# Two feed-forward up projections written as 2x2 block products with seven multiplications

## The chip, the cores and the metric

The kernel runs on one core of one Trainium2 chip. The metric is the device time of one execution in microseconds, the median of several runs; one further execution was profiled, and all rows below come from that one. The core has five engines with a queue each: TensorE (PE, matmuls; its weight loads are listed apart as PEld), VectorE (DVE), ScalarE (ACT), GpSimd (POOL) and SyncE (SP, which here issues the transfers).

## The reference

The model is two layers of a first kind (attention, convolution and retention side by side, then a feed-forward part) followed by one layer of a second kind (differential attention, a state-space branch, then a gated feed-forward part), on one sequence of 512 tokens with width 1024, in float32. The change concerns the feed-forward parts of the second and of the last layer:

```python
# first kind, second layer (D_FF = 4096)
h = rms_norm(x, g_mlp_pre)
f = jnp.square(jax.nn.relu(h @ w_up)) @ w_down
return x + rms_norm(f, g_mlp_post)

# second kind, the last layer (D_FF_2 = 2816)
hn = rmsnorm(h, norm2_gain[i])
up = causal_dwconv(hn @ w_up[i], conv_w[i], conv_b[i])   # 3 taps along the tokens
gate, val = jnp.split(up, 2, axis=-1)
h = h + (jax.nn.silu(gate) * val) @ w_down[i]
```

## The kernel before

All matmuls work on numbers of 128x128 weights by up to 512 columns in the type fp32r. Each float32 operand is split in two such numbers, `hi` (a rounded copy, made by ACT or DVE) and `lo` (the rest, a subtraction, made by DVE or POOL), and a product is the sum of three matmuls: hi by hi, hi by lo, lo by hi (`mm3`).

Weights come as one stream in a fixed order, in chunks of 128 x 1024 numbers (512 KB). A chunk is loaded by SP into a raw buffer (`wraw`, pool `wr`, four buffers), and split into `whi` and `wlo` (pools `wh` and `wl`, four pairs). Other tiles of 128 x 512 come from the pool `sp`. A chunk of an up projection holds 128 output columns for all eight blocks of 128 inputs; its unit (`f_unit`) is 8 x 3 = 24 matmuls of 512 columns (all tokens) into one PSUM bank, and the result has the features on the partitions. The first four units of a feed-forward part are cut in two halves of 256 tokens (`f_split`), so that the first half can run while the last tokens are still being normalised and transposed into `hhi` and `hlo` (`to_hT`). A down projection (`down`) takes four blocks of 128 hidden features at a time and adds 8 outputs (4 token blocks by 2 halves of the width), 12 matmuls of 512 columns each, to an accumulator in SBUF (`acc`, in the last layer the residual `X` itself). So a group of four hidden blocks in the second layer is 4 x 24 + 96 = 192 matmuls, and in the last layer, where every hidden block has a gate and a value unit, 8 x 24 + 96 = 288.

No order is written out by hand beyond that. The program records every operation with a due time (`prio`; evacuations get an earlier one), and `Trace.order` then replays the recording with a table of costs: it picks for each engine the available operation that is due first, chooses among engines where there is a choice (`copy`: ACT or DVE; `sub`: DVE or POOL, with a bias in ns that the stage sets through `wbias`; a bias of 100000 ns keeps POOL out), and takes buffers from the pools. What comes out is a fixed order for each engine. All instructions are issued from one helper line, so every row of the profile has the line L642 (L674 in the changed kernel), and rows are told apart by their tiles.

In the rows, `ps` is a PSUM bank, `t`, `cu` and `cv` are results of up units, `fhi` and `flo` the split hidden features, `st` a column of statistics.

Of the kernel before, what the change touches and what calls it, by code (L numbers as in the profile page):

```python
# [17 lines left out]
P = 128  # L18
S = 512
# [26 lines left out]

def mlp_groups():
    return [(4 * g, 4) for g in range(NG1)]


def ffn2_groups():
    n = DFF2 // 128
    return [(k, min(4, n - k)) for k in range(0, n, 4)]
# [6 lines left out]
def stream_spec():  # L60
    out = []
    for l in range(LAYERS):
# [12 lines left out]
        gs = mlp_groups()  # L75
        for g, (k0, n) in enumerate(gs):
            out += [f_chunk("w_up", l, 128 * (k0 + i)) for i in range(n)]
            if g:
                out += down_chunks("w_down", l, *gs[g - 1])
        out += down_chunks("w_down", l, *gs[-1])  # L80
# [19 lines left out]
    gs = ffn2_groups()  # L100
    for g, (k0, n) in enumerate(gs):
        for i in range(n):
            out.append(f_chunk("w_up_2", 0, 128 * (k0 + i)))
            out.append(f_chunk("w_up_2", 0, DFF2 + 128 * (k0 + i)))
        if g:
            out += down_chunks("w_down_2", 0, *gs[g - 1])
    out += down_chunks("w_down_2", 0, *gs[-1])
# [292 lines left out]
class Trace:  # L400
# [247 lines left out]
    def sub(self, out, a, b, bias=1):  # L648
# [3 lines left out]
        return self.add(alts, (out, a, b), {"op": ALU.subtract})  # L652
# [119 lines left out]

class Side:
# [35 lines left out]
class Builder:  # L809
# [3 lines left out]
    NR, NW = 4, 4  # L813
# [6 lines left out]
    def __init__(self, tc, ctx, A, out):  # L820
# [8 lines left out]
        self.sp = pool("sp", 79 - 2 * self.NR - 4 * self.NW, [P, 512])  # L829
# [8 lines left out]
        self.wbias = 2  # L838

# [23 lines left out]
    def mm3(self, ps, w, a, start, stop):  # L863
        nc = self.nc
        (whi, wlo), (ahi, alo) = w, a
        nc.tensor.matmul(ps, whi, ahi, start=start, stop=False)
        nc.tensor.matmul(ps, whi, alo, start=False, stop=False)
        nc.tensor.matmul(ps, wlo, ahi, start=False, stop=stop)
# [116 lines left out]
    def to_hT(self, t, hs):  # L985
        nc = self.nc
        for h in range(2):
# [4 lines left out]
            self.split(ps.rearrange("p (k n) -> p k n", k=4), self.hhi[sl], self.hlo[sl])  # L992
# [349 lines left out]
    def hybrid(self, l):  # L1342
# [86 lines left out]
        self.side.drain()  # L1429
        self.finish(lambda t: (p0[t],), 4, W_OUT_KS, mix, X, gpost, gpre)  # L1430
        self.mix = {}
        self.mlp(l, X)
# [17 lines left out]
    def mlp(self, l, X):  # L1450
# [35 lines left out]
        self.finish_mlp(groups[-1], lhs, acc, X, gpost, gpre, store)  # L1486
        self.xd = xd

    def down(self, grp, lhs, acc, f, first):
        nc = self.nc  # L1490
        k0, n = grp
        nch = n // 2
        ks = list(range(k0, k0 + n))
        for h in range(2):
            ws = [self.ws.take() for _ in range(nch)]
            for t in range(NT):
                ps = self.ps()
                for c in range(nch):
                    self.t_part(ps, ws[c], ks[2 * c:2 * c + 2], t, 512, lhs, c == 0, c == nch - 1)
                if first:  # L1500
                    if h == 0:
                        acc[t] = [None, None]
                    acc[t][h] = self.s2(name="acc")
                    nc.scalar.copy(acc[t][h], ps)
                else:
                    nc.vector.tensor_tensor(acc[t][h], ps, acc[t][h], op=ALU.add)
        for k in ks:
            f.pop(k)

    def finish_mlp(self, grp, lhs, acc, X, gpost, gpre, store):  # L1510
# [6 lines left out]
        for t in range(NT):  # L1517
# [9 lines left out]
            store(t)  # L1527
        self.pending = hs
# [330 lines left out]
    def second(self):  # L1859
# [139 lines left out]
        hs = {}  # L1999
        for t in range(NT):  # L2000
# [11 lines left out]
    def ffn2(self, X):  # L2012
        nc = self.nc
        f, tg = {}, {}
        self.wbias = 3
        cw, cb = PV["convw2"][0], PV["convb2"][0]

        def unit(i, val):
            c = i + (22 if val else 0)

# [18 lines left out]
        for g, (k0, n) in enumerate(groups):  # L2039
# [4 lines left out]
            for u in us:  # L2044
                self.f_unit(u)
# [42 lines left out]
```

## Time and profile before

| | |
|---|---|
| median of 3 runs | 2135.91 us (2134.16 to 2139.28) |
| the profiled execution | 2135.72 us, of which the span from the first to the last instruction is 2134.0 us |
| TensorE matmuls busy | 2036.2 us (95%) |
| VectorE, ScalarE, GpSimd busy | 1362.7, 931.8 and 727.8 us |
| second layer's feed-forward part | from 907.9 to about 1267.8 us |
| last layer's feed-forward part | from 1767.4 us to the end |

The table is read from the top: the span is the time from the first instruction to the last, a busy time is the union of the recorded instructions of an engine, and the two lower lines say where in the span the stages lie that the change touches. The recorded length of a matmul is longer than its distance to the next one, since matmuls overlap in the array; what a matmul costs is the distance between two starts.

### The profile page before, as it was taken

To read this page: it belongs to the slowest core of one execution; us is meant where nothing else is said; L and a number is where in the kernel's file an instruction comes from. 1 tells how busy PE (TensorE), PEld (TensorE's weight loads), DVE (VectorE), ACT (ScalarE), POOL (GpSimd) and SP (SyncE) were. 2 spreads that over 40 slices of the span, in tenths; PEclk is the share of its full clock that TensorE was granted. 3 is DMA by queue.
4 is the path that set the end of the run, shared out by engine and by line. 5 is a ranking of instruction groups with operands and counts; after the bars stand their busy time and mean duration, and the time that the engine had idled before them with its cause. 6 is when DMAs were issued, how large, how long until landed. Compare 5 with 4: busy or idle time off the path is not lost. (4 is left out here: it accounts for less than half of the span.)

```text
span 2134.0 us, 27037 instructions
## 1 busy us (share of the span) xinstructions
PE 2036.2 (95%) x9964; PEld 1709.2 (80%) x9964; DVE 1362.7 (64%) x2127; ACT 931.8 (44%) x1527; POOL 727.8 (34%) x858
## 2 busy tenths in 40 slices
PE   7999889999999998899999998999999999999999
PEld 7987788778888977688888887677777788888887
DVE  5998795444457998563445473379888546655545
ACT  3377544222234376543233244457568224333322
POOL 3662367970004662300000035854553431000000
PEclk9999999999999999999999999999999999999999
DMA  5423333333242423222333354322324423333322
GB/s 181 129 60 119 109 103 130 111 117 99 79 126 90 129 72 116 79 90 89 98 90 108 99 186 139 91 85 65 98 82 146 164 88 100 99 99 99 97 81 79
DMA packets 85556, 225.16 MB, mean 106 GB/s; under 512 B 10416, under 2 KB 20400, under 8 KB 85424
## 3 DMA queue, kind: packets, MB, share of 16 engines
q1 hardware_dynamic: 85424, 223.43, 32.9%
q8 instruction: 79, 1.29, 0.3%
q14 instruction: 53, 0.43, 0.1%
HBM read 204.25 MB, written 19.14 MB: 105 GB/s over the span
## 5 line engine op out<-in xcount | busy, mean ns | idle before, releaser
L642 POOL TENSOR_TENSOR wlo<-wraw,whi 128x1024 fp32r<-128x1024 f32 (+1 forms) x156 | 367.1, 2361 | 1066.9 <-ACT whi L642 865.7
L642 ACT CAST whi<-wraw 128x1024 fp32r<-128x1024 f32 (+1 forms) x323 | 330.8, 1031 | 702.7 <-PE ps L642 617.8
L642 PE MATMUL ps<-hhi,whi 128*128 128x512 f32 (+1 forms) x1488 | 502.7, 367 | 8.7 <-DVE acc L642 2.8
L642 PE MATMUL ps<-hlo,whi 128*128 128x512 f32 (+1 forms) x1488 | 501.7, 367 | 6.8 <-DVE hlo L642 6.8
L642 PE MATMUL ps<-hhi,wlo 128*128 128x512 f32 (+1 forms) x1488 | 501.4, 366 | 0.4 <-DVE wlo L642 0.3
L642 PEld LDWEIGHTS ps<-hhi,whi 128*128 128x128 f32 x1488 | 273.5, 191 | 52.7 <-issue 5.1
L642 PEld LDWEIGHTS ps<-hlo,whi 128*128 128x128 f32 x1488 | 273.8, 192 | 49.3 <-DVE hlo L642 7.9
L642 PEld LDWEIGHTS ps<-hhi,wlo 128*128 128x128 f32 x1488 | 273.4, 191 | 43.4 <-DVE wlo L642 1.4
L642 DVE TENSOR_TENSOR wlo<-wraw,whi 128x1024 fp32r<-128x1024 f32 x178 | 224.6, 1263 | 109.2 <-ACT whi L642 109.1
L642 PE MATMUL ps<-whi,fhi 128*128 128x512 f32 x688 | 249.0, 391 | 5.1 <-DVE acc L642 2.8
L642 PE MATMUL ps<-whi,flo 128*128 128x512 f32 x688 | 249.3, 390 | 0.0
L642 PE MATMUL ps<-wlo,fhi 128*128 128x512 f32 x688 | 249.2, 391 | 0.0
L642 DVE TENSOR_TENSOR acc<-ps,acc 128x512 f32<-128x512 f32 x112 | 76.5, 687 | 153.0 <-PE ps L642 153.0
L642 PE MATMUL ps<-wlo,hhi 128*128 128x384 f32 (+1 forms) x448 | 157.6, 371 | 3.8 <-POOL wlo L642 3.8
L642 PE MATMUL ps<-whi,hhi 128*128 128x384 f32 (+1 forms) x448 | 155.7, 371 | 0.9 <-ACT whi L642 0.7
L642 PEld LDWEIGHTS ps<-whi,fhi 128*128 128x128 f32 x688 | 129.5, 188 | 32.6 <-DVE acc L642 3.2
L642 PE MATMUL ps<-whi,hlo 128*128 128x384 f32 (+1 forms) x448 | 155.3, 370 | 0.0
L642 PEld LDWEIGHTS ps<-whi,flo 128*128 128x128 f32 x688 | 129.7, 189 | 27.1
L642 PEld LDWEIGHTS ps<-wlo,fhi 128*128 128x128 f32 x688 | 129.8, 189 | 26.9
L642 POOL TENSOR_TENSOR st<-st,mhalf 128x1 f32<-128x1 f32 (+1 forms) x56 | 54.8, 980 | 194.0 <-DVE st L642 192.0
L642 DVE TENSOR_SCALAR t<-ps 128x512 f32<-128x512 f32 x64 | 44.1, 690 | 87.9 <-PE ps L642 87.9
L642 DVE TENSOR_TENSOR X<-ps,X 128x512 f32<-128x512 f32 x56 | 38.6, 689 | 91.7 <-PE ps L642 91.7
(249 smaller groups left out, 3247.5 us busy)
## 6 DMA issues: line engine op xcount, KB each, us to landing
wraw<-in_wst SPq DMA_DIRECT2D x302, 512.0 KB, 3.5
wraw<-in_wst SPq DMA_DIRECT2D x32, 384.0 KB, 3.1
gain<-in_gains SPq DMA_DIRECT2D x20, 256.0 KB, 4.3
X<-in_x SPq DMA_DIRECT2D x16, 256.0 KB, 5.4
xd<-X SPq DMA_DIRECT2D x16, 256.0 KB, 2.0
X<-xd SPq DMA_DIRECT2D x16, 256.0 KB, 5.5
gated<-t SPq DMA_DIRECT2D x16, 256.0 KB, 2.1
gate<-gated SPq DMA_DIRECT2D x16, 256.0 KB, 3.6
```

What stands on the lines that cost most here:

```text
L642: getattr(getattr(self.nc, e), m)(*[r(x) for x in op.args], **{k: r(v) for k, v in op.kw.items()})
```

## The change

In both feed-forward parts, after the first four units, two neighbouring units become one `FastUp`: the second layer takes chunks 2i and 2i+1, the last layer the gate and the value chunk of block i. Weights are cut into 2x2 blocks (inputs 0 to 511 and 512 to 1023, by the two chunks), the activations too (the same two halves of the inputs, by tokens 0 to 255 and 256 to 511). Instead of eight block products there are seven (Winograd's form of Strassen's scheme), each 4 x 3 = 12 matmuls of 256 columns. What is then new:

* four sums of weights per pair of units (`wsum`, and `wraw` in place), each 128 x 512, and splits of 3 1/2 instead of 2 chunks (`take_fast`);
* once per stage, copies of the untransposed numbers (`rawT`), eight sums of activations (`sraw`) and their splits (`fast_in`), one of them written over the second token half of `hhi` and `hlo`;
* two PSUM banks per pair (`pa`, `pb`) into which several products are added one after the other; between two products the running sum is copied or combined with another (`FastUp.out`: `mid`, `cu`), so the next product in a bank waits for that;
* the order (1, 2, then 4 of the pair before, 6, then 3 of the pair before, 5, 7) of `fast_unit`, and `fast_end`, which lets the down projection take up the last two products;
* in the last layer the causal convolution reads SBUF (`cu`) and not PSUM; the bias of both stages keeps the subtractions and sums off POOL;
* in the second layer the residual X is written to DRAM at the start of the stage and read back at its end (`spill`; 8 transfers of 256 KB each way);
* five pairs of weight tiles instead of four, a smaller reserve for dynamic transfers, and 58 instead of 55 tiles in `sp`, for the whole program.

```diff
+def ffn2_plan():
+    out = [("up", 2), ("up", 3)]
+    n = NF2 // 4
+    for g in range(n):
+        i = 4 * g + 4
+        out.append(("up", i))
+        if g == n - 1:
+            out.append(("up", i + 1))
+        out.append(("down", g))
+        if g < n - 1:
+            out += [("up", i + e) for e in range(1, 4)]
+    return out
...
+    def take_fast(self):
...
+        self.load_to(j + 2)
+        x, y = self.raw.pop(j), self.raw.pop(j + 1)
...
+        def split(src, names):
+            if len(names) == 2:
+                hi, lo = b.wh.tile(name="whi"), b.wl.tile(name="wlo")
+            else:
+                hi, lo = b.s2(F32R, "whi"), b.s2(F32R, "wlo")
+            nc.copy(hi, src)
+            nc.sub(lo, src, hi.bitcast(F32), b.wbias)
+            for i, n in enumerate(names):
+                out[n] = hi[:, 512 * i:512 * i + 512], lo[:, 512 * i:512 * i + 512]
+        b.prio(t0)
+        split(x, (1, 2))
+        b.prio(t0 + 3 * b.PROD)
+        z, z4 = b.wr.tile(name="wsum"), b.s2(name="wsum")
+        nc.sum(z[:, L], x[:, L], y[:, L], b.wbias)
+        nc.sum(z[:, R], z[:, L], y[:, R], b.wbias)
+        split(z, (5, 6))
+        b.prio(t0 + 6 * b.PROD)
+        nc.sum(y[:, L], y[:, L], y[:, R], b.wbias)
+        nc.sum(z4, z[:, R], x[:, R], b.wbias)
+        split(y, (7, 3))
+        b.prio(t0 + 8 * b.PROD)
+        split(z4, (4,))
...
+    FIRST = {1, 2, 5}
...
+        self.pa, self.pb = b.ps(), b.ps()
+
+    def run(self, i):
+        self.mm(i, self.pa if i in (1, 6, 7, 4) else self.pb, i in self.FIRST)
+        self.b.evac(self.out, i)
...
+    def mm(self, i, ps, first):
+        whi, wlo = (x.rearrange("p (k m) -> p k m", k=4) for x in self.w.pop(i))
+        for k in range(4):
+            self.b.mm3(ps[:, :256], (whi[:, k, :], wlo[:, k, :]), self.a(i, k), first and k == 0, k == 3,
+                       skip_group_check=not first)
...
+        if i == 1:
+            nc.copy(m0[:, L], pa)
+        elif i == 2:
+            nc.vector.tensor_tensor(g0[:, L], pb, m0[:, L], op=ALU.add)
+        elif i == 6:
+            nc.copy(m0[:, R], pa)
+        elif i == 7:
+            nc.copy(m1[:, L], pa)
+            nc.vector.tensor_tensor(g1[:, R], pb, m1[:, L], op=ALU.subtract)
+        elif i == 4:
+            nc.copy(g0[:, R], pa)
+            self.done(0, g0)
+        elif i == 3:
+            nc.vector.tensor_tensor(g1[:, L], pb, m0[:, R], op=ALU.subtract)
+            self.done(1, g1)
...
-    NR, NW = 4, 4
+    NR, NW = 4, 5
...
-        self.sp = pool("sp", 79 - 2 * self.NR - 4 * self.NW, [P, 512])
+        self.sp = pool("sp", 86 - 2 * self.NR - 4 * self.NW, [P, 512])
...
+    def fast_in(self):
...
+            nc.sub(s1, R[1, j], R[1, j + 2], self.wbias)
+            nc.sub(s2, s1, R[0, j], self.wbias)
+            nc.sum(s4, R[0, j + 2], s2, self.wbias)
+            nc.sub(s3, R[0, j], R[1, j], self.wbias)
+            for i, s in ((6, s2), (5, s1), (3, s4)):
+                hi, lo = self.s2(F32R, "shi"), self.s2(F32R, "slo")
+                nc.copy(hi, s)
+                nc.sub(lo, s, hi.bitcast(F32), self.wbias)
...
+            hi, lo = (z[:, 2 * j:2 * j + 2, 256:512] for z in (self.hhi, self.hlo))
+            v = s3.rearrange("p (k n) -> p k n", k=2)
+            nc.copy(hi, v)
+            nc.sub(lo, v, hi.bitcast(F32), self.wbias)
...
+    def fast_unit(self, u):
+
+        v = self.before
+        for i in (1, 2, -4, 6, -3, 5, 7):
+            if i > 0:
+                u.run(i)
+            elif v:
+                v.run(-i)
+        self.before = u
...
+    def mlp(self, l, X):
+        nc = self.nc
+        self.wbias = 1
+        self.seven = True
+        xm = self.spill(X, f"xm{l}")
...
     def ffn2(self, X):
         nc = self.nc
+        self.wbias = 1
+        self.seven = True
         f, tg = {}, {}
-        self.wbias = 3
...
-    nc = bacc.Bacc("TRN2", target_bir_lowering=False, num_devices=1)
+    nc = bacc.Bacc("TRN2", target_bir_lowering=False, num_devices=1, dynamic_dma_scratch_size=2048)
```

The built order shows where this goes. First VectorE in the middle of the last layer's feed-forward part. Before, one pair of units there is this (two weight splits, four steps of the convolution, the product of gate and value, its split):

```order
L642 TENSOR_TENSOR wlo<-wraw,whi 128x1024
L642 SCALAR_TENSOR_TENSOR cv<-ps,pv,cv 128x511
L642 SCALAR_TENSOR_TENSOR cv<-ps,pv,cv 128x510
L642 TENSOR_TENSOR wlo<-wraw,whi 128x1024
L642 SCALAR_TENSOR_TENSOR cv<-ps,pv,cv 128x511
L642 SCALAR_TENSOR_TENSOR cv<-ps,pv,cv 128x510
L642 TENSOR_TENSOR cv<-cv 128x512
L642 TENSOR_TENSOR flo<-cv,fhi 128x512
```

Now the greater part of one pair reads so, in the same stage:

```order
L674 TENSOR_TENSOR wsum<-wraw 128x512
L674 SCALAR_TENSOR_TENSOR cv<-cu,pv,cv 128x511
L674 TENSOR_TENSOR wsum<-wsum,wraw 128x512
L674 TENSOR_TENSOR cu<-ps,mid 128x256 x2
L674 SCALAR_TENSOR_TENSOR cv<-cu,pv,cv 128x510
L674 TENSOR_TENSOR wraw<-wraw 128x512
L674 TENSOR_TENSOR wlo<-wsum,whi 128x1024
L674 SCALAR_TENSOR_TENSOR cv<-cu,pv,cv 128x511
L674 TENSOR_TENSOR wsum<-wsum,wraw 128x512
L674 SCALAR_TENSOR_TENSOR cv<-cu,pv,cv 128x510
L674 TENSOR_TENSOR wlo<-wraw,whi 128x1024
L674 TENSOR_TENSOR cv<-cv 128x512
```

The sums of weights and the combinations of partial products stand between the steps of the convolution, all on VectorE; none of them went to GpSimd.

Second, VectorE at the start of that stage, from the last transposed tokens (`hlo<-ps,hhi`) on. Before:

```order
L642 TENSOR_TENSOR hlo<-ps,hhi 128x4x128 x3
L642 TENSOR_TENSOR wlo<-wraw,whi 128x1024
L642 SCALAR_TENSOR_TENSOR cv<-ps,pv,cv 128x511
L642 SCALAR_TENSOR_TENSOR cv<-ps,pv,cv 128x510
L642 SCALAR_TENSOR_TENSOR cv<-ps,pv,cv 128x511
```

Now:

```order
L674 TENSOR_TENSOR hlo<-ps,hhi 128x4x128 x2
L674 TENSOR_TENSOR wlo<-wsum,whi 128x512
L674 TENSOR_TENSOR sraw<-rawT 128x512 x2
L674 TENSOR_TENSOR sraw<-sraw,rawT 128x512 x2
L674 TENSOR_TENSOR sraw<-rawT 128x512
L674 TENSOR_TENSOR slo<-sraw,shi 128x512 x3
L674 TENSOR_TENSOR sraw<-rawT,sraw 128x512 x2
L674 TENSOR_TENSOR slo<-sraw,shi 128x512
L674 TENSOR_TENSOR wlo<-wsum,whi 128x1024
L674 SCALAR_TENSOR_TENSOR cv<-ps,pv,cv 128x511
L674 TENSOR_TENSOR wlo<-wraw,whi 128x1024
```

The sums of activations and their splits stand ahead of the first evacuation (`cv`) and ahead of the weights of the first new pair.

Third, TensorE in the middle of the last stage. Before, a unit ends in one bank and the down projection begins in another:

```order
L642 MATMUL ps_16560<-hhi_340,whi_16467 128x512
L642 MATMUL ps_16560<-hlo_341,whi_16467 128x512
L642 MATMUL ps_16560<-hhi_340,wlo_16475 128x512
L642 MATMUL ps_16617<-whi_16517,fhi_16150 128x512
L642 MATMUL ps_16617<-wlo_16526,fhi_16150 128x512
```

Now, where product 6 of a pair (`shi`, `slo`) ends in its bank `ps_17889` and product 7 begins in the same one:

```order
L674 MATMUL ps_17889<-shi_17036,whi_17935 128x256
L674 MATMUL ps_17889<-slo_17049,whi_17935 128x256
L674 MATMUL ps_17889<-shi_17036,wlo_17957 128x256
L674 MATMUL ps_18021<-hhi_355,whi_17923 128x256
L674 MATMUL ps_18021<-hlo_356,whi_17923 128x256
L674 MATMUL ps_17889<-hhi_355,whi_17954 128x256
L674 MATMUL ps_17889<-hlo_356,whi_17954 128x256
```

Between the end of the one product and the start of the next in the same bank stand two matmuls of another pair; the copy of the running sum has to be made in that time.

## Rows read from the trace of the kernel before

**Rows 1.** The page, busy time, share and count of each engine.

```profile
PE 2036.2 (95%) x9964; PEld 1709.2 (80%) x9964; DVE 1362.7 (64%) x2127; ACT 931.8 (44%) x1527; POOL 727.8 (34%) x858
```

**Rows 2.** Busy time by stretch: from, to, length, engines (count), clock, DMA share, GB/s.

```profile
1050.00:1093.50 43.50, 43.50 (x194) 36.03 (x193) 20.53 (x23) 13.19 (x16) 2.63 (x1) 1.00 0.33 97
1830.00:1960.00 130.00, 130.00 (x575) 107.70 (x574) 71.34 (x86) 45.06 (x56) 4.83 (x2) 1.00 0.30 95
```

**Rows 3.** Timeline, TensorE, 512 columns: start, length; 55 steps between these.

```profile
937.21 0.39 PE L642 MATMUL ps<-hhi,whi 128*128 128x512 f32 x1
...
949.68 0.39 PE L642 MATMUL ps<-hlo,whi 128*128 128x512 f32 x1
```

**Rows 4.** Timeline, TensorE, 256 columns (`f_split`, last layer): 60 matmuls between these starts.

```profile
1777.85 0.64 PE L642 MATMUL ps<-hhi,wlo 128*128 128x256 f32 x4
...
1785.05 0.64 PE L642 MATMUL ps<-hhi,wlo 128*128 128x256 f32 x4
```

**Rows 5.** Timeline, VectorE, second layer: the same addition in two successive groups.

```profile
1050.29 0.69 DVE L642 TENSOR_TENSOR acc<-ps,acc 128x512 f32<-128x512 f32 x1 [2.03 <-PE ps L642]
...
1093.81 0.69 DVE L642 TENSOR_TENSOR acc<-ps,acc 128x512 f32<-128x512 f32 x1 [2.03 <-PE ps L642]
```

**Rows 6.** Groups by shape, 1830 to 1960 us: count, busy us, mean ns, idle before.

```profile
L642 DVE TENSOR_TENSOR wlo<-wraw,whi 128x1024 fp32r<-128x1024 f32 x22 | 27.6, 1255 | 24.9 <-ACT whi L642 24.9
L642 ACT CAST whi<-wraw 128x1024 fp32r<-128x1024 f32 x24 | 25.3, 1054 | 65.1 <-PE ps L642 63.4 <-issue 1.7
L642 DVE SCALAR_TENSOR_TENSOR cv<-ps,pv,cv 128x511 f32<-128x511 f32 x16 | 11.9, 745 | 0.0
L642 DVE TENSOR_TENSOR X<-ps,X 128x512 f32<-128x512 f32 x16 | 11.0, 688 | 27.5 <-PE ps L642 27.5
L642 DVE TENSOR_TENSOR flo<-cv,fhi 128x512 fp32r<-128x512 f32 x8 | 5.5, 693 | 5.5 <-ACT fhi L642 5.5
```

**Rows 7.** Groups by shape, whole span: work on PSUM of 512 and 384 columns.

```profile
L642 DVE TENSOR_TENSOR ptlo<-ps,pthi 128x384 fp32r<-128x384 f32 x52 | 26.8, 545 | 0.3 <-ACT pthi L642 0.2
...
L642 ACT CAST pthi<-ps 128x512 fp32r<-128x512 f32 x43 | 24.9, 589 | 46.2 <-PE ps L642 45.4 <-POOL pthi L642 0.3 <-issue 0.3
L642 ACT CAST pthi<-ps 128x384 fp32r<-128x384 f32 x52 | 23.3, 487 | 6.0 <-PE ps L642 4.9 <-POOL pthi L642 0.7
```

**Rows 8.** Timeline, VectorE, an instruction and the next behind it.

```profile
907.37 1.21 DVE L642 TENSOR_TENSOR wlo<-wraw,whi 128x1024 fp32r<-128x1024 f32 x1
908.50 0.15 DVE L642 SCALAR_TENSOR_TENSOR st<-st 128x1 f32<-128x1 f32 x1
```

**Rows 9.** Timeline of a hand-over from TensorE to ScalarE.

```profile
916.98 0.60 PE L642 MATMUL ps<-cm,t 128*128 128x128 f32 x4
917.62 0.59 ACT L642 CAST hhi<-ps 128x512 fp32r<-128x512 f32 x1 [2.45 <-PE ps L642]
```

**Rows 10.** Waits of TensorE: for whom, us in total, times, longest.

```profile
PE ps L642 <- DVE t L642: 19.6, 14, 2.8
...
PE ps L642 <- POOL wlo L642: 3.8, 2, 2.2
...
PE ps L642 <- ACT whi L642: 0.7, 1, 0.7
PE ps L642 <- DVE wlo L642: 0.3, 1, 0.3
```

**Rows 11.** Timeline, TensorE, first layer's feed-forward part: a wait, and what follows.

```profile
385.41 0.47 PE L642 MATMUL ps<-hhi,whi 128*128 128x512 f32 x1 [2.82 <-DVE acc L642]
...
388.10 0.63 PE L642 MATMUL ps<-wlo,fhi 128*128 128x512 f32 x1
388.52 0.63 PE L642 MATMUL ps<-hhi,whi 128*128 128x512 f32 x1
```

**Rows 12.** The page, DMA queues and issues (KB each, us to landing).

```profile
q1 hardware_dynamic: 85424, 223.43, 32.9%
...
X<-xd SPq DMA_DIRECT2D x16, 256.0 KB, 5.5
```

More of the change, by code (lines that the diff above doesn't have):

```diff
@@ L99, in stream_spec @@
         out += t_chunks("w_out_2", 0, ((512 * h, 512),))
[L100 to L107, printed above, removed]
+    up2 = lambda i: [f_chunk("w_up_2", 0, DFF2 * e + 128 * i) for e in range(2)]
+    out += up2(0) + up2(1)
+    for kind, i in ffn2_plan():
+        out += up2(i) if kind == "up" else down_chunks("w_down_2", 0, 4 * i, 4)
+    out += down_chunks("w_down_2", 0, NF2 - 2, 2)
     return out
@@ L994, in run, with fast_end @@
+    def fast_unit(self, u):
[6 more added lines that the diff above has]
+        self.before = u
+    def fast_end(self, steps=(4, 3)):
+        if self.before:
+            for i in steps:
+                self.before.run(i)
+            if 3 in steps:
+                self.before = None
     def run(self):
@@ L1485, in store, with finish_plain @@
                 nc.sync.dma_start(out=xd[t][h], in_=X[t][h])
-        self.finish_mlp(groups[-1], lhs, acc, X, gpost, gpre, store)
+        self.finish_plain(groups[-1], lhs, acc, X, gpost, gpre, store)
         self.xd = xd
[L1489 to L1510, printed above, removed]
+    def finish_plain(self, grp, lhs, acc, X, gpost, gpre, store):
         nc = self.nc
@@ new lines, in down @@
+    def down(self, grp, lhs, acc, f, first):
+        nc = self.nc
+        k0, n = grp
+        nch = n // 2
+        ks = list(range(k0, k0 + n))
+        for h in range(2):
+            ws = [self.ws.take() for _ in range(nch)]
+            for t in range(NT):
+                ps = self.ps(side=self.seven)
+                for c in range(nch):
+                    self.t_part(ps, ws[c], ks[2 * c:2 * c + 2], t, 512, lhs, c == 0, c == nch - 1)
+                if first:
+                    if h == 0:
+                        acc[t] = [None, None]
+                    acc[t][h] = self.s2(name="acc")
+                    nc.scalar.copy(acc[t][h], ps)
+                else:
+                    nc.vector.tensor_tensor(acc[t][h], ps, acc[t][h], op=ALU.add)
+                if h == 0 and t < 2:
+                    self.fast_end((4, 3)[t:t + 1])
+        for k in ks:
+            f.pop(k)
@@ L1999, in second @@
         hs = {}
+        self.rawT = {}
         for t in range(NT):
@@ new lines, in conv @@
+            if not val:
+                nc.scalar.activation(t, t, AF.Silu)
+                tg[i] = t
+                return
+            nc.sub(t, t, tg.pop(i), self.wbias, ALU.mult)
+            hi, lo = self.s2(F32R, "fhi"), self.s2(F32R, "flo")
+            nc.copy(hi, t)
+            nc.sub(lo, t, hi.bitcast(F32), self.wbias)
+            f[i] = hi, lo
+        us = [lambda ps, i=i, v=v: conv(i, v, ps) for i in range(2) for v in (False, True)]
+        self.f_split(us, self.mid_start((1, 3)))
```

220 lines of the change are left out of this document (172 added, 48 removed).

## The prediction

> **What bounds the kernel now.** I first read the engines' busy time: TensorE is busy for 95% of the span, no other engine above 64% [rows 1]. An average hides stages, so I next took the two stages of the change by windows: in a group of the second layer TensorE is busy 43.50 of 43.50 us, in the last layer 130.00 of 130.00, while VectorE has about half and ScalarE a third to do and GpSimd next to nothing [rows 2]. So there the end is set by the number of matmuls and the distance between their starts, and I looked for that distance in TensorE's timeline. With 512 columns it is (949.68 - 937.21) / 55 = 0.2267 us [rows 3]. The check is the period of a whole group: 1093.81 - 1050.29 = 43.52 us for 192 matmuls, again 0.2267 [rows 5]; nothing else is in it. With 256 columns, the width that all new matmuls have, the first units of the last layer show (1785.05 - 1777.85) / 60 = 0.1200 us [rows 4]. Two narrow ones cost 0.2400, not 0.2267: by these two rows 13 ns of each matmul do not depend on its width.
>
> **What is removed.** A pair of units is 48 matmuls of 512 columns, 48 x 0.2267 = 10.88 us. It becomes 7 x 12 = 84 of 256 columns, 84 x 0.1200 = 10.08 us. That is 0.80 us a pair, 7% and not an eighth, since the fixed part is paid 84 times. Pairs: 32 blocks less the first four, by two, are 14 in the second layer; 22 blocks less two are 20 in the last. 34 x 0.80 = **27.2 us**, if TensorE stays as full as it is.
>
> Here the Trainium skill says something else. "TensorE: Matmul & The Clock Gate", section "Back-to-back issue gap", gives a warm distance of N / 2.4 + 2.5 ns, which is 215.8 and 109.2 ns; by it a pair would save 1.19 us and the change 40 us. The trace does not agree: it has 226.7 and 120.0 ns for the same widths, and I take those.
>
> **What is added, and what hides it.** VectorE, per pair of the last layer: four subtractions of 1024 columns (three for the pair, one for the down weights), nine operations of 512 (half a chunk, four sums, gate times value, its split, two additions to X), four steps of convolution, three combinations of 256. The rows give 1.255, 0.69 and 0.745 us for the first three [rows 6]; for 256 I go down the line from 0.688 at 512 to 0.545 at 384, to 0.40 [rows 6, 7]. One starts before the last has ended, 0.08 us here (907.37 + 1.21 against 908.50) [rows 8], and that subtraction undisturbed is 1.13 us from start to start. So between 4 x 1.13 + 9 x 0.61 + 4 x 0.665 + 3 x 0.32 = 13.6 us and, with full lengths, 15.4 us. TensorE needs 10.08 + 24 x 0.2267 = 15.52 us for the same pair. It is covered at both ends, but at the upper one with nothing to spare. I take 13.6, since work that stands ready does follow as in [rows 8]. In the second layer the same sum is 5 x 1.13 + 13 x 0.61 + 3 x 0.32 = 14.5 us, with full lengths 16.5, against 10.08 + 48 x 0.2267 = 20.96: roomy. ScalarE had 45.06 of 130 us [rows 2], 5.7 us in a pair of 16.32; one and a half chunk casts at 1.05 [rows 6] and four copies of 256 columns, 0.385 each by the line from 0.589 to 0.487 [rows 7], make it 8.8 of 15.52: covered.
>
> New are the hand-overs inside a bank. After a product, ScalarE has to copy the sum before the next product may add to it. From the start of the last matmul: its length of 0.28 us (0.64 less three steps of 0.12) [rows 4], 0.04 to ScalarE's start (916.98 + 0.60 against 917.62) [rows 9], the copy of 0.385, and as much again to get back: 0.745, so 0.62 us must be filled by other matmuls. In the built order nearly all places have 0.80 us or more of them. Four, one in each of four groups of the last layer, have two matmuls (0.24 us), as in the third piece of order, and one more has 0.45. That is 4 x 0.38 + 0.17 = 1.7 us of wait that nothing fills. If at those five ScalarE is also in a chunk cast (1.05 us), it is 7. I take **2.0**.
>
> Start of the stages: VectorE now has 16 sums and splits of activations (16 x 0.61 = 9.8 us) in front of the new products. The cover is the second half of the first four units. In the last layer the first product on them stands 162 matmuls, 19.3 us, behind the last transpose, and VectorE has 4.9 us of work up to it. In the second layer product 5 is the tight one: 183 matmuls and 22.8 us, against 19.5 us of VectorE's rows, which begin some 2 us after that transpose. So about 1 us is left there. I take 1 us lost in each stage, **2.0** together; between nothing and, with the cover gone, 2 x 9.8 = 19.6.
>
> At nothing: the 16 transfers of X (5.5 us from issue to landing when read [rows 12]; the reads are issued ahead of the last group of matmuls; without that cover one such time); the smaller reserve, as the page has one dynamic queue, the hardware's [rows 12]; and the order of all the other stages, which the planner lays anew because there are five pairs of weight tiles and 58 other tiles. That can go either way. All of TensorE's waits for weights together are 4.8 us (3.8, 0.7, 0.3), the most that deeper buffers can give. On the other side I allow a quarter of the 19.6 us that it waits for VectorE's `t`, 5 us, as an estimate [rows 10].
>
> The sum against the profiled execution: 2135.72 - 27.2 + 2.0 + 2.0 = 2112.5 us; its span of 2134.0 would become 2110.8. That execution lies 0.2 us below the median of the runs, so the same number stands for it.
>
> **Rivals.**
> *VectorE becomes the bound of the last layer.* For it: 15.4 us with full lengths leaves 0.1 us in a pair, and each operation that waits for another engine loses its overlap. Against it: so far TensorE does not wait for VectorE in this stage at all [rows 2], and weights and sums can be made a pair ahead. If a pair takes 16.0 us, 20 x 0.5 = 10 us are lost, if 16.3, all 16: 2122 to 2128. It begins at 15.52.
> *The start of the stages is not covered.* 19.6 in place of 2.0: 2130. For it: about 1 us is left in the second layer. Against it: in the last layer over 10.
> *Narrow matmuls cost half of wide ones.* Then a pair takes 84 x 0.1133 = 9.52 us, the change saves 34 x 1.36 = 46 us and the time is 2094. For it speaks no row; against it the 60 steps of [rows 4]. The page named above leans to this side.
> *Slower: a wait at each group's hand-over to the down projection.* The down projection needs all four hidden blocks; the last one's chain (two combinations, convolution, product, split) now begins later, from a product of the pair after. There are 7 + 5 such places. A wait of TensorE on VectorE costs 2.82 us in the first layer, and behind it matmuls stood 0.42 apart (388.10, 388.52) and not 0.2267 [rows 11]. At 2.82 in every group it is 33.8 us and the time 2146; it turns the sign at 23.2 / 12 = 1.9 us a group. Against it: down matmuls on the first three blocks, and the next pair's, can run in that time.
> That the change does nothing is excluded: the built program has 84 matmuls where 48 stood.
>
> **How the numbers follow.** The forecast 0.70; its own range is 2105 (1.7 of hand-overs, 2 at the starts, 4.8 gained elsewhere) to 2120 (7 of hand-overs, 5 lost elsewhere, some at the starts). VectorE as the bound 0.12, uncovered starts 0.07, half cost 0.05, slower 0.06. The range 2104 to 2127 takes in the forecast's and nearly all of VectorE's case and leaves out the rest, under 2 in 10. About 0.2% (4.3 us) is what a measurement of this kernel can tell from no change: faster than 2131.4 are the forecast, half cost and nearly all of the two milder cases, 0.89; 0.05 of these end within it; slower 0.06.
>
> **What would show it.** Distances of 0.120 between the new matmuls; a group of 288 in the last layer down from 65.3 us (288 x 0.2267) to about 62.5, and a group of the second from 43.5 to 41.9; VectorE at 85 to 95% in the last stage; short waits of TensorE for ScalarE's `mid`, about 0.4 us, once a group; no long wait on `slo` or `hlo` behind the transposes. Wrong would be: waits on `cu`, `flo` or `wlo` in every group (VectorE is the bound), a clock below 1.00 in these stages, or a changed length of the stages that were not edited.

## The result and the profile after

The changed kernel takes 2104.67 us (median of 4 runs, 2103.2 to 2105.0); the kernel before, run beside it, 2135.16. The ratio is 0.9849 with a 95% interval of 0.9836 to 0.9861. It became faster, as forecast, but by 30.5 us and not by 23.2, and the time lies at the low end of the range: the median 0.7 us inside it, the ratio times 2135.91, 2103.7, 0.3 us outside. The first look is at the engines as in [rows 1], on the page of the changed kernel:

```profile
PE 2015.8 (96%) x11188; PEld 1745.7 (83%) x11188; DVE 1527.6 (73%) x2485; ACT 1042.0 (50%) x1773; POOL 691.8 (33%) x846
```

TensorE's busy time fell by 20.4 us and the span by 30.7, so some 10 us of the gain are TensorE's idle time, which the forecast did not count on. Where? I cut both spans into stages at the last copy of ScalarE into `hhi` in each set of transposes. In order: the entry, the first layer's mixer and feed-forward stage, the second layer's mixer and feed-forward stage, the last layer's mixer and feed-forward stage. Columns as in [rows 2]. Before:

```profile
0.00:29.89 29.89, 16.83 (x115) 15.86 (x116) 16.57 (x22) 13.76 (x28) 13.12 (x12) 1.00 0.77 269
29.89:290.05 260.16, 241.25 (x1307) 213.83 (x1306) 219.98 (x396) 142.27 (x269) 124.04 (x140) 0.97 0.32 99
290.05:667.39 377.34, 363.39 (x1679) 302.56 (x1679) 207.66 (x331) 124.66 (x176) 173.90 (x371) 0.98 0.35 112
667.39:922.40 255.01, 234.29 (x1291) 207.00 (x1291) 209.20 (x346) 138.05 (x262) 112.93 (x131) 0.99 0.29 93
922.40:1281.54 359.14, 355.74 (x1682) 298.62 (x1682) 183.30 (x231) 128.85 (x185) 32.64 (x20) 1.00 0.36 111
1281.54:1776.62 495.08, 471.06 (x2278) 376.06 (x2278) 329.79 (x566) 262.37 (x458) 256.73 (x179) 0.99 0.34 107
1776.62:2134.00 357.38, 353.60 (x1624) 295.30 (x1622) 196.23 (x238) 121.86 (x153) 14.46 (x6) 1.00 0.29 92
```

After:

```profile
0.00:29.60 29.60, 17.40 (x115) 16.43 (x116) 16.52 (x22) 14.59 (x29) 14.94 (x13) 1.00 0.80 274
29.60:282.81 253.21, 235.87 (x1297) 209.41 (x1296) 219.95 (x407) 139.67 (x266) 126.45 (x142) 0.98 0.33 104
282.81:660.94 378.13, 364.93 (x1692) 305.65 (x1691) 203.01 (x320) 124.69 (x176) 169.41 (x369) 0.98 0.36 110
660.94:902.59 241.65, 231.04 (x1270) 204.72 (x1270) 198.10 (x353) 141.25 (x274) 105.90 (x128) 0.99 0.32 99
902.59:1259.68 357.09, 352.85 (x2218) 319.61 (x2217) 254.64 (x380) 170.24 (x279) 17.30 (x15) 0.99 0.40 126
1259.68:1752.54 492.86, 471.85 (x2266) 374.15 (x2265) 334.94 (x571) 268.23 (x470) 257.85 (x180) 0.99 0.34 104
1752.54:2103.20 350.66, 341.90 (x2342) 315.79 (x2340) 300.39 (x436) 183.32 (x284) 0.00 (x0) 1.00 0.29 95
```

The two edited stages, the fifth and the last, are only 2.1 and 6.7 us shorter. The two mixers of the first kind, in which no line of work was edited, are 6.9 and 13.4 us shorter. The last thing that the prediction named as a sign against itself, a changed length of the unedited stages, is the main thing that happened. Some 20 matmuls of 256 and 384 columns moved over a cut from one stage to the next, so one to three us of a difference can be a matter of bookkeeping.

In the second layer's mixer the waits of TensorE changed owner and length. Before, the longest of them (for whom, us in total, times, longest):

```profile
PE ps L642 <- DVE row L642: 5.7, 4, 1.9
PE ps L642 <- DVE t L642: 2.6, 2, 1.7
PE ps L642 <- DVE st L642: 2.1, 1, 2.1
PE ps L642 <- DVE klo L642: 1.7, 2, 1.4
PE ps L642 <- POOL wlo L642: 1.7, 1, 1.7
```

After:

```profile
PE ps L674 <- DVE row L674: 3.4, 3, 1.6
PE ps L674 <- DVE hlo L674: 2.1, 1, 2.1
PE ps L674 <- DVE rotb L674: 1.5, 1, 1.5
```

Only 1.5 us of what went were booked as waits for weights (`wlo`, 1.7 to 0.2); the rest were waits for VectorE's `t`, its statistics (`row`, `st`) and split operands. VectorE is as busy as before in the first mixer (219.98 and 219.95 us), so it was not relieved of work there.

### The profile page after: what moved, and what is told of

It reads as the page before. It is cut to its first block, busy times and chain, and to the rows that moved or that the text cites. A ratio compares the mean times of both kernels' runs of the same rounds, so it can differ in the third digit from the quotient of the medians.

```text
span 2103.3 us, 29992 instructions
## 1 busy us (share of the span) xinstructions
PE 2015.8 (96%) x11188; PEld 1745.7 (83%) x11188; DVE 1527.6 (73%) x2485; ACT 1042.0 (50%) x1773; POOL 691.8 (33%) x846
## 5 line engine op out<-in xcount | busy, mean ns | idle before, releaser
L674 POOL TENSOR_TENSOR wlo<-wraw,whi 128x1024 fp32r<-128x1024 f32 (+1 forms) x144 | 337.1, 2347 | 526.3 <-ACT whi L674 433.6
L674 PE MATMUL ps<-hhi,whi 128*128 128x256 f32 (+1 forms) x1488 | 454.9, 331 | 7.2 <-ACT hhi L674 2.3
L674 PE MATMUL ps<-hlo,whi 128*128 128x256 f32 (+1 forms) x1488 | 452.3, 329 | 9.6 <-DVE hlo L674 9.6
L674 PE MATMUL ps<-hhi,wlo 128*128 128x256 f32 (+1 forms) x1488 | 449.8, 328 | 1.2 <-DVE wlo L674 1.2
L674 DVE TENSOR_TENSOR wlo<-wraw,whi 128x1024 fp32r<-128x1024 f32 x190 | 235.8, 1247 | 59.7 <-ACT whi L674 59.5
L674 PE MATMUL ps<-wlo,fhi 128*128 128x512 f32 x688 | 251.9, 392 | 1.6 <-DVE wlo L674 1.6
L674 PE MATMUL ps<-shi,whi 128*128 128x256 f32 (+1 forms) x440 | 124.3, 292 | 0.6 <-ACT mid L674 0.6
L674 PE MATMUL ps<-slo,whi 128*128 128x256 f32 (+1 forms) x440 | 124.2, 291 | 0.0
L674 PE MATMUL ps<-shi,wlo 128*128 128x256 f32 (+1 forms) x440 | 124.0, 290 | 0.0
```

The lines of the kernel that those rows point to most:

```text
L674: getattr(getattr(self.nc, e), m)(*[r(x) for x in op.args], **{k: r(v) for k, v in op.kw.items()})
```

## The experiments

**Theory A:** the extra gain comes from the buffers. Five pairs of weight tiles and 58 other tiles let the planner lay another order for the whole program. **Theory B:** it comes from the seven-product stages, which change what the planner can pull into the mixers next to them. Beside that, the seven-product form itself gave less than 27.2 us, and the question was which of its terms was wrong. Each kernel was run beside the kernel before, whose medians lay between 2135.06 and 2137.24 in these sets of runs; differences of 2 us or less between two of them are therefore not told apart.

**e1, the buffers alone.**

```diff
--- before
-    NR, NW = 4, 4
+    NR, NW = 4, 5
...
-        self.sp = pool("sp", 79 - 2 * self.NR - 4 * self.NW, [P, 512])
+        self.sp = pool("sp", 86 - 2 * self.NR - 4 * self.NW, [P, 512])
...
-    nc = bacc.Bacc("TRN2", target_bir_lowering=False, num_devices=1)
+    nc = bacc.Bacc("TRN2", target_bir_lowering=False, num_devices=1, dynamic_dma_scratch_size=2048)
```

> The kernel before, with only the smaller transfer reserve, five pairs of weight tiles and 58 other tiles; no seven-product form anywhere. Stages are cut where ScalarE makes its last hhi copy of a set of transposes. In the changed kernel the unedited stages became 22.0 us shorter (6.9 in the first layer's mixer, 13.4 in the second layer's mixer, 2.2 in the last mixer, -0.5 in the rest) and the two edited ones 8.7. Theory A (the new order that the planner lays with more buffers gives the 22 us): this kernel takes about 2114 us, with the first mixer near 253 and the second near 242 us. Theory B (the mixers gain only because the seven-product stages behind or ahead of them changed what the planner may pull in): the first mixer may still gain its 7, the second mixer stays near 255 us, and the kernel takes 2127 to 2136 us.

2118.21 us, ratio 0.992 (0.9905 to 0.9935). In this kernel the first two mixers and, below them, the second layer's and the last layer's feed-forward stages are:

```profile
29.62:282.69 253.07, 235.58 (x1297) 209.12 (x1296) 219.89 (x407) 139.61 (x266) 126.28 (x142) 0.98 0.32 104
659.30:904.15 244.85, 231.99 (x1274) 205.00 (x1274) 198.59 (x349) 138.23 (x261) 111.43 (x130) 0.99 0.31 98
904.15:1267.87 363.72, 358.92 (x1709) 301.66 (x1709) 185.09 (x233) 127.97 (x184) 34.72 (x21) 1.00 0.35 110
1759.42:2115.90 356.48, 352.76 (x1617) 294.36 (x1615) 195.05 (x237) 120.76 (x152) 14.47 (x6) 1.00 0.28 90
```

The mixers are those of the changed kernel but for 3 us. Theory A holds for the greater part: **16.9 us of the 30.5 come from buffers and order, 13.5 (2118.21 - 2104.67) from the seven products.** Beside this kernel the two edited stages of the changed one are 6.6 and 5.8 us shorter, not 2.1 and 6.7: the buffers alone make the second layer's feed-forward stage longer, 363.72 us against 359.14, with some of the matmuls that the mixer ahead of it gave up.

**e2, four pairs of weight tiles under the seven products** (`NR, NW = 4, 4` in the changed kernel; `sp` then has 62 tiles).

> The changed kernel with four pairs of weight tiles instead of five; the 8 tiles' room goes to the pool sp (66 - 4 = 62 tiles). Theory A with the fifth pair as its cause: the mixers fall back to 260 and 255 us and the time rises by about 20 us, to 2125 us, and more if the seven-product stages, which keep 3 1/2 chunks of a pair in work, then wait for wlo. Theory A with the other tiles as its cause: the time stays within 4 us of 2104.7. Theory B: the mixers keep 253 and 242 us; only the edited stages may get longer.

2118.9 us. The second mixer falls back to 252.2 us, the first has 254.8, and the last stage takes 359.3 us, longer than the plain form does (356 to 357 in e1, e4 and before): TensorE now waits there for the rounded weights and for the running sum.

```profile
PE ps L674 <- ACT whi L674: 4.9, 5, 1.4
PE ps L674 <- ACT mid L674: 2.2, 6, 0.8
PE ps L674 <- DVE cu L674: 1.6, 2, 0.8
```

So with only four pairs the new form's gain in the last layer is gone, and more than that. The plain form with the same buffers (e5 below) has nearly the same mixers, 254.6 and 253.2 us: with four pairs they hang on the buffers and hardly on the form. Against e5 the seven products give 8.1 us (2126.99 - 2118.9), and the stage in which they do is the second layer's, 351.8 us against 359.2.

**e3 and e4, the seven products in one layer only.**

```diff
--- after (e3)
-FAST = (1,)
+FAST = ()
--- after (e4)
-        self.rawT = {}
...
     def ffn2(self, X):
...
```

In e4 the body of `ffn2`, its order of chunks and its bias are those of the kernel before.

> The changed kernel with the seven-product form in the last layer only; the second layer's feed-forward stage runs the plain form without the spill of X. By the prediction's own pitch sum the 14 pairs of the second layer are worth 14 x 0.80 - 1.0 = 10.2 us, so 2114.9 us. By the stage lengths of the changed kernel they are worth 2.1 us in their own stage: theory A (mixers gain by buffers alone) gives 2106.8 us with the second mixer at 242 us; theory B (the second mixer's 13.4 us hang on the seven-product stage behind it) gives 2104.7 + 2.1 + 13.4 = 2120 us.

> The changed kernel with the seven-product form in the second layer only; the last feed-forward stage runs the plain form with the old stream order and bias. By the prediction's pitch sum the 20 pairs of the last layer are worth 16.0 us less 2.0 of hand-overs and 1.0 at the start, 13.0, so 2117.7 us. By the stage length of the changed kernel they are worth 6.6 us: 2111.3 us, if the last mixer stays as it is. Both theories leave the first two mixers as in the changed kernel (253 and 242 us).

2111.67 and 2109.06 us. e3 falls between the numbers of theories A and B: the second mixer has 244.8 us here, as in e1, so 3 of its 13.4 us do hang on the stage behind it (four matmuls fewer and 2 us less idle time in the mixer). Against e1 the second layer's form is worth 9.2 us (2118.21 - 2109.06) and the last layer's 6.5; with the other one present they are worth 7.0 and 4.4. The forecast had 10.2 and 13.0. So the second layer is nearly as forecast, and the last one gives a third to a half.

**e5 to e7, the three buffer edits apart** (the kernel before with the smaller reserve and: 62 other tiles; five pairs and 55 tiles; nothing else).

> The kernel before with the smaller transfer reserve and its room given to the pool sp alone: four pairs of weight tiles, 62 other tiles instead of 55. The three buffer edits together took 16.9 us off. If the other tiles are the cause, this kernel takes about 2118 us and the first two mixers are near 253 and 245 us; if the fifth pair is, it takes about 2135; if each has a share, one mixer shortens and the other does not (the changed kernel with four pairs and 62 tiles had 254.8 and 252.2 us, which speaks for the first mixer by tiles, the second by the pair: then 2127 to 2130).

> The kernel before with the smaller transfer reserve, five pairs of weight tiles and the old 55 other tiles. Fifth pair as the cause: about 2118 us, mixers 253 and 245. Other tiles as the cause: about 2135. A share each, the second mixer by the pair: 260 and 245 us, 2124 to 2127.

> The kernel before with only the smaller transfer reserve, pools as before, so that each engine's order is that of before. If the reserve itself costs or gives time through the transfers, the time moves; if, as the prediction has it, it is worth nothing, 2135 us within 0.2% and every stage length as before.

2126.99 (ratio 0.9965, 0.9953 to 0.9978), 2132.61 (0.9988, 0.9979 to 0.9998) and 2135.6 (1.0000, 0.9990 to 1.0009). The reserve itself is worth nothing. Tiles alone give 8.1 us and the pair alone 2.5, together 16.9: they do not add. That each has a share fits for the tiles (2127 to 2130 expected) and not for the pair, with which the mixers have 257.2 and 251.9 us, not the 260 and 245 guessed. (The profiled execution of e5, 2122.68 us, was its fastest by 3.8.)

**e8, GpSimd allowed for the down weights of the last stage** (and for the chunks of its first four units, which are split in the same place). The stage of the changed kernel is 5.9 us shorter than the plain one (356.6 in e4, 350.7), not 13. Its waits:

```profile
PE ps L674 <- DVE wlo L674: 2.8, 4, 1.2
PE ps L674 <- ACT mid L674: 1.6, 6, 0.6
PE ps L674 <- ACT cu L674: 0.6, 1, 0.6
```

A wait costs more than its own length. TensorE's timeline at a hand-over inside a bank and at a down projection that waits for `wlo` (start, length, and in brackets the wait):

```profile
1845.85 0.28 PE L674 MATMUL ps<-hlo,whi 128*128 128x256 f32 x1
1846.36 0.38 PE L674 MATMUL ps<-hhi,whi 128*128 128x256 f32 x1 [0.23 <-ACT mid L674]
1846.58 0.28 PE L674 MATMUL ps<-hlo,whi 128*128 128x256 f32 x1
1846.70 0.28 PE L674 MATMUL ps<-hhi,wlo 128*128 128x256 f32 x1
...
1854.85 1.09 PE L674 MATMUL ps<-whi,fhi 128*128 128x512 f32 x4
1856.47 0.50 PE L674 MATMUL ps<-wlo,fhi 128*128 128x512 f32 x1 [0.53 <-DVE wlo L674]
1856.81 0.40 PE L674 MATMUL ps<-whi,flo 128*128 128x512 f32 x1
1857.04 0.40 PE L674 MATMUL ps<-whi,fhi 128*128 128x512 f32 x1
1857.37 0.38 PE L674 MATMUL ps<-shi,whi 128*128 128x256 f32 x1
1857.59 0.28 PE L674 MATMUL ps<-slo,whi 128*128 128x256 f32 x1
1857.71 0.28 PE L674 MATMUL ps<-shi,wlo 128*128 128x256 f32 x1
```

The upper piece: starts 0.51 and 0.22 apart where 0.12 is the rule (the distance in an undisturbed stream), 0.49 us lost for a wait shown as 0.23. The lower piece: 1.62 for four matmuls of 0.2267, then, with one of 0.23 among them, 0.34, 0.33 and 0.22 where 0.227, 0.227 and 0.12 are the rule, 1.0 us lost for 0.53. Summed over the last stage so (every distance above its rule) the loss is 9.1 us: 2.2 at the start, 2.2 at hand-overs, 4.7 with `wlo` (three down projections with 1.0 each, and 1.7 once within a pair).

```diff
--- after, in prep_to (gated is set in ffn2)
-            nc.sub(lo[:, :n], t[:, :n], hi[:, :n].bitcast(F32), b.wbias)
+            nc.sub(lo[:, :n], t[:, :n], hi[:, :n].bitcast(F32), 3 if b.gated else b.wbias)
```

> The changed kernel, but in the last stage the subtraction that splits a chunk of down weights may go to GpSimd, as it could before. In the changed kernel TensorE loses 9.1 us in that stage to waits and what follows them, against 3.0 in the prediction; the longest are on VectorE's wlo, ahead of each down projection. If VectorE is too busy there (the prediction's first rival, in part), taking these subtractions off it removes the wlo waits and the stage falls from 350.6 to about 347, the time to 2101. If the wait comes only from the order in which VectorE takes its work, or if GpSimd's 2.35 us instead of 1.2 makes wlo late in turn, the time stays within 0.1% of 2104.7 or grows.

2112.21 us, 7.5 slower. The last stage takes 359.4 us, and TensorE waits 7.5 us for VectorE's `cu`. The cause stands in the two engines' timelines, GpSimd first:

```profile
1917.01 2.57 POOL L674 TENSOR_TENSOR wlo<-wraw,whi 128x1024 fp32r<-128x1024 f32 x1 [48.30 <-ACT whi L674]
```

```profile
1917.24 2.89 DVE L674 TENSOR_TENSOR wraw<-wraw 128x512 f32<-128x512 f32 x1
1920.05 0.68 DVE L674 TENSOR_TENSOR cv<-cv 128x512 f32<-128x512 f32 x1
```

VectorE's sum of two operands in SBUF, 0.68 us alone, started 0.23 us behind GpSimd's subtraction and ended 0.55 us after it. It stood still until GpSimd was done. The Trainium skill says so ("SBUF — State Buffer", section "Who interferes with whom"): a VectorE instruction with two inputs in SBUF and a GpSimd instruction that reads SBUF exclude each other, and the later one waits; this trace agrees. So it went with each of the 14 subtractions that GpSimd took in this stage: one VectorE instruction with two operands in SBUF that started behind it ended 0.55 us after it (1.08 us the one of 1024 columns), while `cu<-ps,mid`, which has one operand in PSUM, took 0.41 to 0.42 us in the same stretches. VectorE was spared 14 x 1.22 = 17.1 us and held up for 24.7, and its busy time in the stage rose from 300.4 to 308.8 us.

**e9, VectorE relieved in the last stage:** two of the three taps of the convolution are left out, so this kernel does not compute the reference.

```diff
--- after, in conv
-            nc.vector.scalar_tensor_tensor(t[:, 1:], src[:, :511], w[1], t[:, 1:], op0=ALU.mult, op1=ALU.add)
-            nc.vector.scalar_tensor_tensor(t[:, 2:], src[:, :510], w[0], t[:, 2:], op0=ALU.mult, op1=ALU.add)
```

> The changed kernel without the two VectorE steps of the causal convolution (two of its three taps are left out) in all blocks of the last layer that come from a gate or value unit, so VectorE has about 2.7 us less per pair of units. TensorE's losses in the last stage of the changed kernel, waits with the slower matmuls behind them, are 9.1 us: 2.1 at the stage's start, 2.2 at hand-overs inside a bank (mid), 4.7 where the down projection waits for wlo. If VectorE's load is what makes wlo late, the 4.7 go and the stage falls from 350.6 to 346 us, the time to 2100; the waits on mid, which are ScalarE's, stay. If only the order in which VectorE serves its work makes wlo late, most of the 4.7 stays and the time is 2103 to 2105.

2092.57 us; the last stage takes 341.5 us and TensorE waits in it for nothing, not even for `mid`, which was to stay. So this run took away more than VectorE's load: less work is also another order, and it can't tell the two apart.

**e10 and e12, the planner told the measured pitch**, with the seven products and without.

```diff
-            return max(0.4222 * n, 107.0) + 2.5 if n >= 192 else 213.0
+            return 0.4168 * n + 13.3 if n >= 192 else 213.0
```

> The changed kernel, with the planner's cost of a matmul set to the measured pitch (0.4168 ns per column and 13.3 ns: 226.7 at 512, 120.0 at 256) instead of 0.4222 ns per column and 2.5 ns (218.7 and 110.6). If the waits that are left come from an order laid for a TensorE faster than the real one, the waits on wlo and mid shrink and the time falls by 3 to 8 us, to 2097 to 2102. If the order depends on small differences in a way that nothing steers, as the buffers' effect suggests, the stages move by a few us in both directions and the time lies anywhere within 8 us of 2104.7.

> The kernel before with the three buffer edits (2118.2 us) and the planner's matmul cost set to the measured pitch; no seven-product form. If a true cost makes a better order, this kernel also gains 3 to 8 us, to 2110 to 2115. If the order is an accident, it lies within 8 us of 2118.2 on either side, and its sign need not be that of the same edit in the changed kernel.

2140.1 and 2167.32 us: the truer number makes the program 35 and 49 us slower. The work is the same. In e12 the mixers have 263.9, 254.0 and 510.3 us (e1: 253.1, 244.9 and 491.6). The guess of 8 us either way was far too small. Idle time is the smaller part of it. The last mixer, in e12 and then in e1:

```profile
1298.91:1809.18 510.27, 483.71 (x2287) 380.32 (x2287) 334.90 (x562) 263.54 (x459) 261.31 (x181) 0.97 0.32 103
1267.87:1759.42 491.55, 470.93 (x2271) 373.73 (x2270) 332.54 (x565) 265.03 (x458) 263.49 (x182) 0.99 0.34 107
```

The three mixers of e12 have as many matmuls as those of e1 (4842) and take 38.7 us longer. Of these, 15.9 are idle time of TensorE, and 22.8 are longer busy time, at a mean granted clock of 0.96, 0.98 and 0.97 against 0.98, 0.99 and 0.99. In e10 the last stage, however, has 343.3 us, 7.3 fewer than in the changed kernel, with 0.6 us of idle time ahead of its last matmul.

**e11, one more tile** (59 in `sp`).

> The changed kernel with one more tile in sp, 59. If room is what the mixers were short of, one more tile gives a small gain, about 1 us (seven tiles alone gave 8.1), and no stage gets longer. If the gain of the buffers is an accident of the new order, the mixers change by some us either way, up to the 8 that the fifth pair with the old number of tiles lost again.

2101.72 us, 3 us less by medians; the ratio, 0.9839 (0.9824 to 0.9853), overlaps that of the changed kernel, so the gain is not sure. In the profile the second mixer went from 241.7 to 239.0 us, and no stage became longer by more than 0.7.

**e13, the measured pitch in the last stage alone** (`op.real` is set for all that `ffn2` records).

```diff
+            if op.real and n >= 192:
+                return 0.4168 * n + 13.3
             return max(0.4222 * n, 107.0) + 2.5 if n >= 192 else 213.0
```

> The changed kernel, with the measured pitch as the planner's cost of a matmul in the last feed-forward stage alone; all stages ahead of it keep the order of the changed kernel. With that cost everywhere the stage took 343.3 us and TensorE idled 0.6 us in it, against 350.6 and 5.1. If the stage's loss is one of order, it takes about 343 us again and the time is 2097.4. If VectorE had no room for the order to use (capacity), or if the shorter stage came from its other entrance, it stays near 350 and the time near 2104.7.

2098.43 us, ratio 0.9821 (0.9805 to 0.9838). The last stage, and all of TensorE's waits in it:

```profile
1752.82:2096.10 343.28, 338.96 (x2333) 315.25 (x2331) 296.51 (x434) 182.75 (x283) 0.00 (x0) 1.00 0.30 97
```

```profile
PE ps L675 <- DVE cv L675: 0.4, 1, 0.4
```

VectorE does the same work (296.5 us busy, 300.4 in the changed kernel), 86% of the stage, GpSimd none, and TensorE waits once, for 0.4 us. Summed as above, its loss in the stage is 2.5 us instead of 9.1. The greater part of the loss was one of order, not of VectorE's capacity.

**e14 and e15, on from e13:** 59 tiles; and a cost 4.5 ns lower than before in all stages ahead of the last.

> The same with 59 tiles in sp instead of 58. If the two gains (3.0 us by the 59th tile, all of it ahead of the last stage, and 7.3 us in the last stage) add, 2094.4 us; if the last stage's order changes with the tile count as the mixers' does, anywhere between 2094 and 2102.

> The changed kernel with the measured pitch in the last stage, and in all stages ahead of it a matmul cost 4.5 ns lower than before (214.2 at 512 columns, 106.1 at 256), further from the truth. Raising it by 8 to 9.4 ns to the truth made the mixers and the first feed-forward stage some 42 us longer. If the order follows the size of that cost (the lower, the better the mixers fill), the stages ahead shorten by 5 to 20 us and the time falls below 2092. If each order is an accident of its numbers, the stages ahead move by up to 10 us either way, most likely longer.

2092.21 (ratio 0.9793, 0.9779 to 0.9808) and 2093.14 us. In e14 the two gains add (12.5 us against 3.0 and 6.2; the rest is within the noise). By its median it is the fastest version that computes the whole reference, 44 us below the kernel before (2136.52 beside it), though the 1 us to e15 tells nothing. e15 gained too, but not as a rule would have it: against e13 the second mixer became 3.4 us longer, the first feed-forward stage 3.0 and the last mixer 3.3 shorter.

## Why the prediction was right in sign and wrong in size

**The failed step** is the one "at nothing", the order of all the other stages. It was bounded by -4.8 and +5 us; it measured -16.9 (e1). The lower bound was "all of TensorE's waits for weights", as if deeper buffers could only shorten waits that the trace books on weights; in e1 those fell by 3.6 us, from 4.8 to 1.2. But a buffer here is a condition in the planner: with more of them it starts other work sooner, all engines' orders change, and every wait is in play: in e1 those for `klo` fell from 5.2 to 0.9 us and those for `gt`, `mixlo` and `kb`, 9.2 together, went, while `t` and `row` did not fall (37.0 to 42.8, 7.3 of it a wait in the entry that before was booked on a transfer). A better bound on that term was the idle time of TensorE in the stages that are not full, some 90 us in the table of stages before. It is not a strict one: of the 18.1 us by which e1's span is shorter (2134.0, 2115.9), 5.2 are TensorE's busy time (2036.2, 2031.0). That there is no sign to it is shown by e12: the same program with another number in the planner lost 49.

**The seven-product form was put too high**, 23.2 us against 13.5 measured, so that the two errors partly cancel; that the time came out so near the range is luck. The lower end of the forecast's own range was added up wrongly besides: 1.7 of hand-overs, 2 at the starts and 4.8 gained elsewhere make 2107.4 us and not 2105, which takes nothing lost at the starts. By its terms:

* *Pitch.* Right. In the second layer the same addition starts 42.09 us later in the next group, with nothing between; compare [rows 5], 43.52:

```profile
1015.02 0.68 DVE L674 TENSOR_TENSOR acc<-ps,acc 128x512 f32<-128x512 f32 x1
...
1057.11 0.69 DVE L674 TENSOR_TENSOR acc<-ps,acc 128x512 f32<-128x512 f32 x1
```

  41.9 was forecast. Between new matmuls the distance is 0.120; a wide one ahead of a narrow one takes 0.233 and not 0.2267, and this mixing costs the 0.1 to 0.2 us a group. That narrow matmuls might cost half is out. The Trainium skill's rule that leaned to that side ("TensorE: Matmul & The Clock Gate", section "Back-to-back issue gap", 0.109 us for 256 columns) isn't borne out by the 0.120 here; the section gives it for a single isolated matmul, and not for a stream in which every matmul has its own weight load, as here.
* *Second layer.* 10.2 forecast, 7.0 to 9.2 measured (e3, e4). No wait at its start, where 1.0 was put, and 0.4 us lost up to 1228 us, summed as for the last stage. On the way into the next mixer TensorE waits 1.7 us for `t` and 1.9 for `x`, nearly as in e1 (1.6 and 1.6), but from 1230 to 1260 us at a mean granted clock of 0.83 (some 10 us at the lower of its two levels, 0.50), where e1 has 1.00 in the stretch that answers to it. In e11, with 0.94 there, the stage takes 355.8 us instead of 357.1; no run isolates what the clock costs.
* *Last layer.* 13.0 forecast, 4.4 to 6.5 measured. Hand-overs inside a bank: 2.0 forecast, 2.2 measured, at four places of 0.49 and one smaller, as read from the built order; each distance was 0.385 too long, where 0.38 stood, and the next one 0.10. Start: 1.0 forecast, 2.2 measured, so the 2.0 for both starts came out by luck. **Waits for `wlo`, most of them at the down projection: nothing forecast, 4.7 measured.** The 16.0 of the pitch less these 9.1 are 6.9, near what was measured. A group takes 63.72 us (the same addition to X) where 62.5 was forecast:

```profile
1872.14 0.68 DVE L674 TENSOR_TENSOR X<-ps,X 128x512 f32<-128x512 f32 x1
...
1935.86 0.69 DVE L674 TENSOR_TENSOR X<-ps,X 128x512 f32<-128x512 f32 x1
```

**The rivals.** VectorE as the bound: in its load the forecast was good (55.43 of 63.70 us in that group, 87%, where 85 to 95% stood), and VectorE's queue did make TensorE wait, but e13 shows that the same load fits with hardly a wait, and then the stage is 13.2 us shorter than the plain one (356.48 in e1, 343.28), the 13.0 of the forecast. What was missing in the step is the question in which order VectorE takes its work. In the changed kernel, ahead of the down projection shown above, it ran without a pause from 1848.93 us on, and the subtraction for which TensorE waited was the last of that run:

```profile
1848.93 0.43 DVE L674 TENSOR_TENSOR cu<-ps,mid 128x256 f32<-128x256 f32 x1 [0.83 <-PE ps L674]
...
1854.59 0.69 DVE L674 TENSOR_TENSOR wsum<-wsum,wraw 128x512 f32<-128x512 f32 x1
1855.19 1.22 DVE L674 TENSOR_TENSOR wlo<-wraw,whi 128x1024 fp32r<-128x1024 f32 x1
```

A sum of weights for a pair stood just ahead of it. Uncovered starts (19.6 us) did not happen: 2.2 in the last layer and nothing in the second. The slower case did not happen either: nothing waits at the hidden block's chain, only at the weights.

**The other signs.** Short waits on `mid` were there, 0.2 to 0.6 us. There was no long wait on `slo` or `hlo` behind the transposes. Of the signs against the forecast, changed lengths of unedited stages were there; waits on `wlo` came in three of the last stage's groups, not in every one; and the clock was below 1.00 at the end of the second layer's stage.

**Still open** is why the old, too small cost gives the better mixers. e11, e12, e13 and e15 show that single numbers move a stage by up to 19 us up and 7 us down; they show no rule by which to choose them, and none was found.

## What to carry to other kernels

Where a planner lays the order of a whole program, a change of buffers or of a cost is a change of every stage: bound it by no less than the idle time of all stages that are not full, not by the waits that are booked on the buffer, and run the buffers alone before crediting the arithmetic. When an edit puts new work on an engine that is not the bound, compare its busy share with the order in which it serves what the bound waits for; at 86% busy both 0.4 and 5 us of TensorE's waits were possible with the same instructions. A number that is nearer to the truth can give a worse order, so test it stage by stage and keep it where it helps.

## What was not expected of the hardware

A short wait of TensorE costs 0.26 to 0.5 us more than it shows, in the matmuls around it: 0.49 lost for 0.23, and 1.0 for 0.53, where three of the next four distances too were 0.10 to 0.11 longer, all at a granted clock of 1.00 in that stretch. By these rows 0.16 us of it is overlap: a matmul's record (0.28 or 0.39 us) outlasts its distance to the next (0.12 or 0.227) by as much, and a wait is counted only from the record's end. The slower matmuls behind it stay unexplained. And GpSimd's help can be dearer than none: 14 subtractions in the last stage of e8 made single VectorE instructions of 0.68 us last up to 2.89.
